# A four-layer hybrid model on one Trainium2 core: the residual stream by tokens instead of by features, and the FFN's output product by seven products of quarters

## The chip, the cores and the metric

The kernel runs on one core of one Trainium2 chip. The metric is the device time of one execution in microseconds. Before the change it was 2659.95 us, the median of three runs (2656.53 to 2660.51).

## The reference, cut to what matters

512 tokens of width 1024 go through four layers. Each layer is a mixer (RWKV-7, sliding-window attention, a gated spatial unit, gated linear attention) and an FFN, each behind an RMS norm and added to the residual stream `h`. All is float32.

```python
for i in range(DEPTH):                       # DEPTH = 4
    hn = rmsnorm(h, norm_mix[i])
    m = [rwkv7_mix, swa_sink_mix, sgu_chunk_mix, gla_mix][i](hn, ...)
    h = h + m
    h = h + swiglu(rmsnorm(h, norm_ffn[i]), ffn_w_in[i], ffn_w_out[i])
return rmsnorm(h, norm_final)

def rmsnorm(x, g):                           # over the 1024 features of a token
    return x * lax.rsqrt(jnp.mean(jnp.square(x), -1, keepdims=True) + 1e-5) * g
def swiglu(x, w_in, w_out):                  # w_in 1024 x 5632, w_out 2816 x 1024
    gate, up = jnp.split(x @ w_in, 2, axis=-1)
    return (jax.nn.silu(gate) * up) @ w_out
```

## The kernel before, in words

**Products.** A float32 product is made of three fp32r matmuls: each operand is split into a high part (a cast on ScalarE) and a low part (the rest, a subtraction on VectorE), and `mm3` multiplies high by high, high by low and low by high. Weights come by DMA into `wraw` tiles of 128 x 1024 (pool `wr`, eight buffers) and are split into `whi` and `wlo` (pools `wh` and `wl`, three buffers each).

**Residual stream.** `h` lies by features: eight tiles of 128 features x 512 tokens, two in each buffer of the pool `hp`. `out_proj` goes over the eight feature tiles: `gemm` multiplies one with the weights as the stationary operand and 512 tokens moving, `residual` adds the PSUM bank to `h[n]`, and after a stage's last product `norm_tile` prepares the next norm of that tile: a square on ScalarE, an add of it into the tile `acc` on GpSimd, and the scaled operand `h * g`, split in two. `rstd` then transposes `acc` by four blocks on PE, reduces it on VectorE, and takes the reciprocal root by three Newton steps; the factor per token is applied later, to results.

**FFN.** Its hidden width of 2816 is cut into six blocks (`WIDTHS`: four of 512, two of 384), and the blocks into three parts of two (`PARTS`). `hidden` makes gate and up of a block by `seven`: with input features and tokens halved, the four quarters of the weights (gate and up by feature half) and of the input give eight products, of which seven of sums of quarters suffice (the Strassen-Winograd scheme). The products are called m1, m2, m5, m6, m3, m7, m4 in the order made, with left operands x11, x12, s5, s6, s3, s7, x22. Sums of weight quarters are made by accumulating DMAs, issued by GpSimd: raw tile `b` takes quarters 2, 0, 3 and 1 one after another, tile `c` takes 3 and then 2. Left operands for an input are made once, by `fast_tile`, when the norm is prepared (`fast`). m1, m6, m7 and m4 accumulate in the same two PSUM banks and are read between. After each part, `out_proj` multiplies its hidden features by all eight k-tiles (six in the last part), in the plain way.

**Order.** Instructions are recorded as a program; `Program.run` puts each engine's in an order of its own by simulating the engines with a price per instruction (`price`): among ready instructions it takes the one that starts earliest, by program order within 60 ns. Up to 700 instructions ahead may be moved forward, if buffers allow. `keep_warm` fills idle PE time with products of the identity. All instructions are issued from line 233 (those fillers from line 453), so the profile's groups are told apart by tile names: `slot` are general 128 x 512 tiles (46 of them, `SLOTS`), `left` those of the FFN's results, `ps` the eight PSUM banks.

Of the kernel before, what the change touches and what calls it, by code (L numbers as in the profile page):

```python
# [17 lines left out]
P = 128  # L18
# [7 lines left out]
SLOTS = 46  # L26
# [7 lines left out]
VECS = ("norm_mix", "rw_mu", "rw_w0", "rw_a0", "rw_k_k", "rw_k_a", "rw_r_k", "norm_ffn", "norm_final", "sw_b_qkv", "sw_b_o", "sg_b_u", "sg_b_o", "gla_b_a",  # L34
# [402 lines left out]
class K:  # L437
# [3 lines left out]
    def __init__(self, prog, d, es):  # L441
# [16 lines left out]
        self.nx = []  # L458
        self.fast = False
# [13 lines left out]
    def stream(self, slots):  # L473

        self.acc = self.pool("acc", 1, side="right").tile([P, S], F32, name="acc")
        self.weight_pools(8, 3, side="right")
        self.big = self.pool("big", slots, side="right")
# [6 lines left out]
    def load_x(self, h):  # L484
        for k in range(KT):
            self.nc.sync.dma_start(h[k], self.d['x_t'][k * P:(k + 1) * P, :])

# [83 lines left out]
    def norm_tile(self, k, g):  # L571

        nc = self.nc
        last = g is self.v['norm_final']
        if k == 0:
            nc.scalar.activation(self.acc, self.h[k], AF.Square)
        else:
            sq = self.slot()
            nc.scalar.activation(sq, self.h[k], AF.Square)
            (nc.vector if last else nc.gpsimd).tensor_add(self.acc, self.acc, sq)  # L580
        if last:
            self.nx.append(self.slot())
            nc.scalar.activation(self.nx[k], self.h[k], AF.Identity, scale=g(k))
            return
        if self.fast:
            self.fast_tile(k, g)
            return
        xh, xl = self.pair()
        nc.scalar.activation(xh, self.h[k], AF.Identity, scale=g(k))
        nc.vector.scalar_tensor_tensor(xl, self.h[k], g(k), xh, op0=ALU.mult, op1=ALU.subtract)  # L590
        self.nx.append((xh, xl))

    def fast_tile(self, k, g):

        nc = self.nc
        x = self.slot()
        nc.scalar.activation(x, self.h[k], AF.Identity, scale=g(k))
        j, H = k % 4, S // 2  # L600
        a, b = slice(0, H), slice(H, S)
        if k < 4:
            if k % 2 == 0:
                self.x11 = self.pair()
            c = slice(k % 2 * H, k % 2 * H + H)
            one = tuple(t[:, c] for t in self.x11)
            self.split(x[:, a], *one)
            self.nx.append([one, x])
            return
        one, y = self.nx[j]  # L610
        two = self.pair()
        self.split(x, *two)
        f, g = self.slot(), self.slot()
        nc.vector.tensor_sub(f[:, a], x[:, b], y[:, b])
        nc.vector.scalar_tensor_tensor(f[:, b], f[:, a], -1.0, y[:, a], op0=ALU.mult, op1=ALU.subtract)
        nc.vector.tensor_sub(g[:, a], y[:, a], y[:, b])
        nc.vector.scalar_tensor_tensor(g[:, b], f[:, b], -1.0, x[:, a], op0=ALU.mult, op1=ALU.subtract)
        fs, gs = self.pair(), self.pair()
        self.split(f, *fs)
        self.split(g, *gs)  # L620
        half = lambda p, c: tuple(t[:, c] for t in p)
        self.nx[j] = dict(x11=one, x12=half(two, a), x22=half(two, b), s5=half(fs, a), s6=half(fs, b), s7=half(gs, a), s3=half(gs, b))
# [13 lines left out]
    def rstd(self, copy=True, spread=True):  # L636

        nc = self.nc
        ps = self.bank()
        for b in range(NB):  # L640
            nc.tensor.transpose(ps[:, b * P:(b + 1) * P], self.acc[:, b * P:(b + 1) * P], self.ident)
        ms = self.sm.tile([P, NB], F32, name="ms")
        nc.vector.tensor_reduce(ms, self.blocks(ps), axis=AX.X, op=ALU.add)
# [8 lines left out]
        if not copy:  # L652
            return col, ps
# [4 lines left out]
    def operand(self):  # L658
        x, self.nx = self.nx, []
        return x  # L660

    def residual(self, k, ps, bias=None):
        nc = self.nc
        if bias is None:
            nc.vector.tensor_add(self.h[k], ps, self.h[k])
        else:
            nc.vector.scalar_tensor_tensor(self.h[k], ps, bias, self.h[k], op0=ALU.add, op1=ALU.add)


    def ffn(self, i, g_next):  # L670


        nc, d = self.nc, self.d
        col, _ = self.rstd(spread=False)
        neg = self.sm.tile([P, NB], F32, name="ncol")
        nc.vector.tensor_scalar(neg, col, -1.0, None, op0=ALU.mult)
        x = self.operand()
        done = 0
        for n, part in enumerate(PARTS):
            gs = []  # L680
            for j in part:
                w = d['ffn_w_a'][i, j] if j < 4 else d['ffn_w_b'][i, j - 4]
                m = WIDTHS[j] // P
                oo = [self.pair() for _ in range(m)]
                gs += oo
                self.hidden(w, WIDTHS[j], x, col, neg, oo)
            last = n == len(PARTS) - 1
            self.out_proj(d['ffn_w_out'][i][:, :, done * P:(done + len(gs)) * P], gs, None, g_next if last else None)
            done += len(gs)

    def seven(self, w, W, x):
# [7 lines left out]
        nc = self.nc  # L699

        def load(q):
            t = []
            for u in range(2):
                raw = self.wr.tile([P, 1024], F32, name="wraw")[:, :2 * W]
                nc.sync.dma_start(raw, w[q * 2 + u])
# [3 lines left out]
        def add(a, q):  # L709
            for u in range(2):  # L710
                nc.gpsimd.dma_start(a[u], w[q * 2 + u], accum_op=ALU.add)

        def mm(key, ps, raw, first, last):
            for u in range(2):
                hi = self.wh.tile([P, 1024], F32R, name="whi")[:, :2 * W]
                lo = self.wl.tile([P, 1024], F32R, name="wlo")[:, :2 * W]
                self.split(raw[u], hi, lo)
                for b in range(2):
                    t = slice(b * P, (b + 1) * P)
                    for k in range(2):  # L720
                        xh, xl = x[u * 2 + k][key]
                        c = slice(k * W, (k + 1) * W)
                        self.mm3(ps[b], xh[:, t], xl[:, t], hi[:, c], lo[:, c], first and u + k == 0, last and u + k == 2)
# [27 lines left out]
    def hidden(self, w, W, x, col, neg, oo):  # L751
# [10 lines left out]
        def give(up, half):  # L762
# [3 lines left out]
            for j0 in range(0, W // P, 2):  # L766
# [5 lines left out]
                for j in range(n):  # L772
                    c = slice(half * 256, half * 256 + 256)
                    self.split(ps[:, j * 256:j * 256 + 256], oo[j0 + j][0][:, c], oo[j0 + j][1][:, c])
        for name, ps in self.seven(w, W, x):
# [22 lines left out]
    def out_proj(self, w, x, bias, g_next):  # L798
        for n in range(KT):
            def ev(ps):  # L800
                self.residual(n, ps, bias(n) if bias else None)
                if g_next is not None:
                    self.norm_tile(n, g_next)
            self.gemm(w[n], x, ev)
# [31 lines left out]
    def rwkv(self, g, g_next, slots):  # L836
# [24 lines left out]
        self.acc = self.slot()  # L861
# [829 lines left out]
```

## Time and profile before

| | before |
|---|---|
| median of three runs | 2659.95 us |
| profiled execution, its own time | 2662.47 us |
| its span, first to last instruction | 2660.6 us |
| instructions | 34154 |
| PE busy | 2566.0 us, 12950 products and transposes |
| VectorE, ScalarE, GpSimd busy | 1669.7, 1233.9, 434.3 us |
| granted PE clock, mean | 0.989 |
| moved by DMA | 318.47 MB, of which 92.29 MB by GpSimd's queue |

Busy times are unions of an engine's recorded durations; matmuls overlap, so the distance between starts, not the mean duration, is the price of one. In the windows, each row has the busy time of PE, PE's weight loads, VectorE, ScalarE and GpSimd with their instruction counts, then the granted clock, the DMA engines' mean share and GB/s.

### The profile page before, as it was taken

Reading aid. Unit: us, or ns where it says so; the run is one execution under the profiler, and the core shown is the slowest. Engines: PE = TensorE matmul, PEld = TensorE weight load, DVE = VectorE, ACT = ScalarE, POOL = GpSimd, SP = SyncE. Lnnn points to the kernel's source line nnn. Section 1 sums busy time; section 2 is a strip of 40 time slices with the busy share of each in tenths; the row PEclk is TensorE's granted clock in tenths of the full one; section 3 lists DMA queues with packets and bytes.
Section 4 is the critical chain, followed back from the end, with each engine's and each line's share of the span. In section 5 each row is a group of like instructions: output and inputs, shape, how many; then the busy total and the mean of one; then the engine's idle time right before and its main releaser. Section 6 shows DMA issues by size and latency. Waiting matters only on the chain. (4 is left out here: it accounts for less than half of the span.)

```text
span 2660.6 us, 34154 instructions
## 1 busy us (share of the span) xinstructions
PE 2566.0 (96%) x12950; PEld 2101.2 (79%) x12950; DVE 1669.7 (63%) x2591; ACT 1233.9 (46%) x2047; POOL 434.3 (16%) x431
## 2 busy tenths in 40 slices
PE   8999889979999999999999999999999999999998
PEld 7677677768889865788898888888888777788897
DVE  8686787576466766855556474764646645764555
ACT  4545443356354555644444232553535523553443
POOL 1022343221111233201111000110111000211010
PEclk9999999999999999999999999999999999999999
DMA  3210001168576521667674222384856221576662
GB/s 126 78 60 11 7 9 38 43 161 201 141 176 155 141 81 43 153 182 180 149 179 155 96 88 94 103 199 139 203 126 167 88 72 64 138 186 153 172 151 78
DMA packets 108580, 318.47 MB, mean 120 GB/s; under 512 B 12016, under 2 KB 19568, under 8 KB 108416
## 3 DMA queue, kind: packets, MB, share of 16 engines
q1 hardware_dynamic: 80768, 224.01, 25.5%
q0 software_dynamic: 27648, 92.29, 19.9%
q8 instruction: 101, 1.65, 0.3%
q14 instruction: 63, 0.52, 0.1%
HBM read 311.80 MB, written 2.10 MB: 118 GB/s over the span
## 5 line engine op out<-in xcount | busy, mean ns | idle before, releaser
L233 PE MATMUL ps<-whi,slot 128*128 128x512 f32 (+1 forms) x3328 | 996.9, 378 | 4.2 <-ACT left L233 3.0
L233 ACT CAST whi<-wraw 128x1024 fp32r<-128x1024 f32 (+3 forms) x566 | 558.3, 987 | 844.3 <-PE ps L233 675.3
L233 DVE TENSOR_TENSOR wlo<-wraw,whi 128x1024 fp32r<-128x1024 f32 (+2 forms) x562 | 645.6, 1149 | 409.8 <-ACT whi L233 407.0
L233 PE MATMUL ps<-slot,whi 128*128 128x512 f32 x2784 | 871.1, 392 | 1.6 <-ACT slot L233 1.6
L233 PEld LDWEIGHTS ps<-whi,slot 128*128 128x128 f32 x3328 | 617.4, 188 | 99.5 <-ACT left L233 4.8
L233 PE MATMUL ps<-wlo,slot 128*128 128x512 f32 (+1 forms) x1664 | 627.9, 377 | 4.3 <-DVE wlo L233 4.0
L233 PEld LDWEIGHTS ps<-slot,whi 128*128 128x128 f32 x2784 | 515.6, 187 | 122.6 <-issue 7.0
L233 PE MATMUL ps<-slot,wlo 128*128 128x512 f32 x1392 | 544.0, 391 | 0.0
L233 PEld LDWEIGHTS ps<-wlo,slot 128*128 128x128 f32 x1664 | 312.8, 188 | 57.7 <-DVE wlo L233 11.5
L233 PEld LDWEIGHTS ps<-slot,wlo 128*128 128x128 f32 x1392 | 259.8, 187 | 57.8 <-issue 2.5
L233 DVE TENSOR_TENSOR h<-ps,h 128x512 f32<-128x512 f32 x128 | 88.4, 691 | 283.9 <-PE ps L233 283.8
L233 POOL DMA_DIRECT2D wraw<-ffn_w_a x128 | 111.1, 868 | 655.2 <-DVE wlo L233 345.0
L233 POOL TENSOR_TENSOR acc<-acc,slot 128x512 f32<-128x512 f32 x49 | 74.2, 1514 | 654.3 <-ACT slot L233 654.2
L233 DVE TENSOR_TENSOR slot<-slot 128x512 fp32r<-128x512 f32 (+8 forms) x177 | 131.6, 754 | 23.3 <-ACT slot L233 21.2
L233 ACT COPY left<-ps 128x512 f32<-128x512 f32 (+1 forms) x196 | 108.2, 555 | 78.3 <-PE ps L233 78.2
L233 DVE TENSOR_TENSOR slot<-ps,slot 128x256 fp32r<-128x256 f32 (+3 forms) x271 | 98.3, 416 | 69.3 <-PE ps L233 41.1
L233 POOL DMA_DIRECT2D wraw<-ffn_w_b x64 | 55.2, 864 | 383.8 <-DVE wlo L233 184.7
L233 ACT CAST slot<-ps 128x256 fp32r<-128x256 f32 (+1 forms) x240 | 65.6, 365 | 46.1 <-PE ps L233 41.8
L233 DVE SCALAR_TENSOR_TENSOR left<-left,ncol 128x512 f32<-128x512 f32 (+1 forms) x96 | 65.4, 701 | 9.9 <-ACT left L233 9.9
L233 ACT CAST slot<-slot 128x512 fp32r<-128x512 f32 (+1 forms) x80 | 45.8, 576 | 48.4 <-DVE slot L233 47.6
L233 PE MATMUL ps<-slot 64*128 64x256 f32 (+4 forms) x256 | 58.3, 406 | 7.8 <-DVE slot L233 5.3
L233 DVE TENSOR_TENSOR left<-ps,left 128x512 f32<-128x512 f32 (+1 forms) x96 | 58.4, 638 | 7.9 <-PE ps L233 7.9
(257 smaller groups left out, 2359.0 us busy)
## 6 DMA issues: line engine op xcount, KB each, us to landing
wraw<-ffn_w_a SPq DMA_DIRECT2D x128, 512.0 KB, 3.5
wraw<-ffn_w_a POOLq DMA_DIRECT2D x128, 512.0 KB, 5.7
wraw<-ffn_w_out SPq DMA_DIRECT2D x64, 512.0 KB, 4.0
wraw<-ffn_w_b SPq DMA_DIRECT2D x64, 384.0 KB, 3.1
wraw<-ffn_w_b POOLq DMA_DIRECT2D x64, 384.0 KB, 6.2
wraw<-ffn_w_out SPq DMA_DIRECT2D x32, 384.0 KB, 4.7
wraw<-sg_w_v SPq DMA_DIRECT2D x16, 512.0 KB, 3.6
wraw<-sg_w_u SPq DMA_DIRECT2D x16, 512.0 KB, 3.3
```

Source lines behind the costliest of these rows:

```text
L233: op = self.add(eng.name, lambda: getattr(eng.target, what)(*map(real, args), **{k: real(a) for k, a in kw.items()}), *self.price(eng.name ...
```

## The change

`h` becomes token-major: four tiles of 128 tokens x 1024 features, loaded from `x`, and the kernel's output is token-major too. Output products of the mixers go by `gemm_tok` (tokens stationary, 512 weight columns moving, all k-tiles into four banks); the rwkv one by 256 columns and two k-tiles at a time. Biases are added as broadcast rows by GpSimd at a mixer's start. The FFN's output product goes through `seven` too, with tokens halved, the part's hidden features halved (one block each) and output features halved; its left operands are made per part from the hidden results, and each of the seven results is added to or subtracted from one quarter of `h`. Norms: `finish` takes the square sums of two token blocks and 512 features with ScalarE's accumulated output, and makes the next stage's features by PE transposes of `h` into PSUM, scaled on ScalarE. `acc`, `norm_tile` and `residual` go. `SLOTS` is 48 and the pool `left` 16.

```diff
-SLOTS = 46
+SLOTS = 48
...
+    def finish(self, half, nh):
...
+        c = slice(nh * S, nh * S + S)
+        bs = (2 * half, 2 * half + 1)
+        for b in bs:
             sq = self.slot()
+            nc.scalar.activation(sq, self.h[b][:, c], AF.Square, accum_out=self.ss[:, 2 * b + nh:2 * b + nh + 1])
+        if self.kind == 'final':
+            for b in bs:
+                nc.vector.tensor_mul(self.h[b][:, c], self.h[b][:, c], self.g[nh])
             return
+        t = slice(half * 256, half * 256 + 256)
+        for u in range(2):
+            ps = self.bank()
+            for j in range(2):
+                k = nh * 4 + u * 2 + j
+                for i, b in enumerate(bs):
+                    nc.tensor.transpose(ps[:, (j * 2 + i) * P:(j * 2 + i + 1) * P], self.h[b][:, k * P:(k + 1) * P], self.ident)
...
+                xh, xl = self.nx[k]
+                nc.scalar.activation(xh[:, t], src, AF.Identity, scale=self.g(k))
+                nc.vector.scalar_tensor_tensor(xl[:, t], src, self.g(k), xh[:, t], op0=ALU.mult, op1=ALU.subtract)
+        if self.kind == 'fast':
+            self.quarter(self.xq, self.nf, (nh, half), keep=True)
...
+    def combine(self, q, name):
...
+        x11, x12, x21, x22 = q[0, 0], q[1, 0], q[0, 1], q[1, 1]
+        if name == 's5':
+            q['s'] = [self.slot()[:, :t.shape[-1]] for t in x21]
+        for u in range(len(x11)):
+            if name == 's5':
+                nc.vector.tensor_sub(q['s'][u], x22[u], x21[u])
+            elif name == 's6':
+                nc.vector.scalar_tensor_tensor(q['s'][u], q['s'][u], -1.0, x11[u], op0=ALU.mult, op1=ALU.subtract)
+            elif name == 's3':
+                nc.vector.scalar_tensor_tensor(q['s'][u], q['s'][u], -1.0, x12[u], op0=ALU.mult, op1=ALU.subtract)
+            else:
+                nc.vector.tensor_sub(x21[u], x11[u], x21[u])
+        return x21 if name == 's7' else q['s']
...
+            w = d['ffn_o_a'][i, n] if n < 2 else d['ffn_o_b'][i]
+            self.out_fast(w, W // P, lambda key: self.left_of(gs, key), n == len(PARTS) - 1)
...
+    def out_fast(self, w, nsub, x, last):
...
+        where = {'m1': [(0, 0, 1)], 'm2': [(0, 0, 1)], 'm5': [(1, 1, -1)], 'm6': [(0, 1, -1)], 'm3': [(0, 1, -1)],
+                 'm7': [(1, 1, -1)], 'm4': [(1, 0, 1)]}
+        for name, ps in self.seven(w, S, x, nsub):
+            for half, nh, sign in where[name]:
+                for b in range(2):
+                    c = self.h[half * 2 + b][:, nh * S:(nh + 1) * S]
+                    (nc.vector.tensor_add if sign > 0 else nc.vector.tensor_sub)(c, c, ps[b])
+                if last and name in ('m2', 'm3', 'm7', 'm4'):
+                    self.finish(half, nh)
...
-                    self.split(ps[:, j * 256:j * 256 + 256], oo[j0 + j][0][:, c], oo[j0 + j][1][:, c])
...
+                t = self.slot()[:, :n * 256]
+                nc.scalar.copy(t, ps[:, :n * 256])
+                gs.setdefault((kh, half), []).append(t)
...
+    def out_proj(self, w, x, last=True):
...
+        for nh in range(2):
+            c = slice(nh * S, nh * S + S)
+
+            def ev(b, ps):
+                self.nc.vector.tensor_add(self.h[b][:, c], ps, self.h[b][:, c])
+                if last and b % 2:
+                    self.finish(b // 2, nh)
+            self.gemm_tok(w, nh * S, x, ev)
...
     def store(self):
...
+        col, _ = self.rstd(spread=False)
+        for b in range(NB):
+            for nh in range(2):
+                c = slice(nh * S, nh * S + S)
+                o = self.slot()
+                if nh:
+                    nc.scalar.activation(o, self.h[b][:, c], AF.Identity, scale=col[:, b:b + 1])
+                else:
+                    nc.vector.tensor_scalar(o, self.h[b][:, c], col[:, b:b + 1], None, op0=ALU.mult)
+                nc.sync.dma_start(self.d['out'][b * P:(b + 1) * P, c], o)
```

More of the change, by code (lines that the diff above doesn't have):

```diff
@@ new lines, in finish, with parts, quarter @@
+        if self.kind == 'fast':
+            self.quarter(self.xq, self.nf, (nh, half), keep=True)
+    LEFT = {(0, 0): 'x11', (1, 0): 'x12', (1, 1): 'x22'}
+    def parts(self, ts):
+        out = []
+        for t in ts:
+            n = t.shape[-1]
+            hi, lo = self.pair()
+            self.split(t, hi[:, :n], lo[:, :n])
+            out.append((hi[:, :n], lo[:, :n]))
+        return out
+    def quarter(self, q, out, key, keep):
+        if key in self.LEFT:
+            out[self.LEFT[key]] = self.parts(q[key])
+        if len(q) == 4 and all(len(v) == len(q[0, 0]) for v in q.values()):
+            for n in ('s5', 's6', 's7', 's3'):
+                out[n] = self.parts(self.combine(q, n))
@@ L967, in rwkv @@
                 ahead(n + 1)
-        self.h = self.eight()
-        self.load_x(self.h)
+        self.load_h()
         self.rwkv_out_proj(oo, 0, 6)
@@ L974, in rwkv @@
         self.stream(slots)
[L975 to L980 removed]
+        self.begin(g_next)
+        self.out_proj(d['rw_w_o'][6 * P:, :], oo[6:])
         ex.close()
```

281 lines of the change are left out of this document (120 added, 161 removed).

## The prediction

> **What bounds the kernel now.** I read the page first, then the windows cut at the stage boundaries, then the timeline inside one FFN, then the groups, the DMA issues and the chain of waits.
>
> ```profile
> span 2660.6 us, 34154 instructions
> ...
> PE 2566.0 (96%) x12950; PEld 2101.2 (79%) x12950; DVE 1669.7 (63%) x2591; ACT 1233.9 (46%) x2047; POOL 434.3 (16%) x431
> ```
>
> PE is busy nearly always, so a gain has to come from PE's work or from the 95 us in which it idles. The windows (columns: stretch, its length, busy time of each engine, granted clock, DMA share, GB/s) tell where those are:
>
> ```profile
> 594.00:620.00 26.00, 25.25 (x109) 20.74 (x110) 16.34 (x21) 16.01 (x23) 4.29 (x5) 0.93 0.88 199
> 620.00:880.00 260.00, 260.00 (x1247) 223.00 (x1246) 149.81 (x196) 120.44 (x175) 33.51 (x41) 1.00 0.69 164
> 880.00:910.00 30.00, 29.68 (x146) 25.36 (x145) 21.17 (x30) 15.88 (x28) 3.92 (x3) 1.00 0.54 173
> 910.00:1075.00 165.00, 155.06 (x721) 107.63 (x720) 114.45 (x214) 90.97 (x248) 57.56 (x49) 1.00 0.23 71
> 1075.00:1140.00 65.00, 63.12 (x287) 51.70 (x286) 52.26 (x78) 41.58 (x60) 14.56 (x14) 1.00 0.71 173
> ...
> 1700.00:1765.00 65.00, 63.29 (x288) 52.05 (x287) 51.18 (x77) 42.22 (x59) 15.12 (x14) 1.00 0.68 166
> ...
> 2280.00:2340.00 60.00, 57.86 (x260) 47.17 (x259) 47.17 (x71) 36.98 (x52) 13.08 (x13) 1.00 0.67 156
> ```
>
> The body of an FFN (620 to 880) has PE busy for 260.00 of 260 us while VectorE stands at 58%, ScalarE at 46% and DMA at 0.69. The passage from an FFN into a mixer (880 to 910) loses 0.3 us. The passage from a mixer into an FFN (the four windows around 600, 1100, 1730, 2310) loses 0.75, 1.88, 1.71 and 2.14 us, 6.5 together: there the square sums in acc end late. So an FFN is bound by the number of PE instructions, and the price of one is its distance from the next:
>
> ```profile
> 779.31 1.23 DVE L233 TENSOR_TENSOR wlo<-wraw,whi 128x1024 fp32r<-128x1024 f32 x1 [0.20 <-ACT whi L233]
> ...
> 780.46 1.05 ACT L233 CAST whi<-wraw 128x1024 fp32r<-128x1024 f32 x1 [1.18 <-PE ps L233]
> ...
> 784.71 0.69 PEld L233 LDWEIGHTS ps<-ident,left 128*128 128x128 f32 x6 [0.17 <-DVE left L233]
> 784.82 0.82 PE L233 MATMUL ps<-ident,left 128*128 128x128 f32 x6
> ...
> 787.30 0.62 PE L233 MATMUL ps<-slot,whi 128*128 128x512 f32 x2
> ...
> 787.75 0.39 PE L233 MATMUL ps<-slot,wlo 128*128 128x512 f32 x1
> ...
> 787.98 0.62 PE L233 MATMUL ps<-slot,whi 128*128 128x512 f32 x2
> ```
>
> Three 512-column products lie between 787.30 and 787.98: 0.227 us each. Six transposes' weight loads take 0.69 us: 0.115 each, or 0.11 from start to start when the last one's own length (140 ns, group row below) is taken off and the rest divided by five.
>
> **The change, PE first.** (a) An FFN's output product took 22 k-tiles x 8 output tiles x 3 = 528 products of 512 columns. By quarters it is 7 x 2 token blocks x (4+4+3) k-tiles x 3 = 462. Four FFNs: 264 fewer x 0.227 = -59.9 us, all of it on PE's path, since nothing else ends last there. (b) Features now come by transposes: 32 at each of the seven norms that feed a stage, 224 x 0.11 = +24.6. (c) Four transposes of acc at each of eight norms and four that spread the final column go: 36 x 0.11 = -4.0. Net -39.3 us. The mixers' output products keep their count (192 for 8 k-tiles either way). The rwkv one becomes 288 products of 256 columns for 144 of 512. A product of 256 columns is not in the trace; half of 0.227 is 0.113 and a weight load can follow the last after 0.11, so I take 0, with 144 x 0.11 = 16 us as the far end should weight loads hold it up.
>
> **What the other engines get.** The groups (busy, mean ns of one, idle before and its releaser):
>
> ```profile
> L233 DVE TENSOR_TENSOR slot<-slot 128x512 fp32r<-128x512 f32 (+8 forms) x177 | 131.6, 754 | 23.3 <-ACT slot L233 21.2
> L233 DVE TENSOR_TENSOR slot<-ps,slot 128x256 fp32r<-128x256 f32 (+3 forms) x271 | 98.3, 416 | 69.3 <-PE ps L233 41.1 <-ACT slot L233 28.0
> L233 DVE TENSOR_TENSOR h<-ps,h 128x512 f32<-128x512 f32 x128 | 88.4, 691 | 283.9 <-PE ps L233 283.8
> L233 POOL TENSOR_TENSOR acc<-acc,slot 128x512 f32<-128x512 f32 x49 | 74.2, 1514 | 654.3 <-ACT slot L233 654.2
> L233 ACT CAST slot<-ps 128x256 fp32r<-128x256 f32 (+1 forms) x240 | 65.6, 365 | 46.1 <-PE ps L233 41.8 <-DVE slot L233 4.1
> L233 PEld LDWEIGHTS ps<-ident,left 128*128 128x128 f32 x352 | 43.2, 140 | 11.1 <-DVE left L233 3.0
> L233 ACT ACTIVATE slot<-h 128x512 f32<-128x512 f32 x57 | 35.9, 630 | 19.4 <-DVE h L233 16.8 <-DMA h<-x_t 1.5
> ```
>
> VectorE's recorded durations overlap, as its own timeline shows:
>
> ```profile
> 878.63 0.95 DVE L233 TENSOR_TENSOR wlo<-wraw,whi 128x768 fp32r<-128x768 f32 x1
> 879.49 0.55 DVE L233 TENSOR_TENSOR left<-ps,left 128x384 f32<-128x384 f32 x1
> 879.96 1.14 DVE L233 SCALAR_TENSOR_TENSOR left<-left,ncol 128x384 f32<-128x384 f32 x2
> ...
> 883.92 1.08 DVE L233 TENSOR_TENSOR slot<-ps,slot 128x256 fp32r<-128x256 f32 x3
> 884.92 1.01 DVE L233 TENSOR_TENSOR left<-left 128x384 f32<-128x384 f32 x2
> ...
> 893.97 0.69 DVE L233 TENSOR_TENSOR h<-ps,h 128x512 f32<-128x512 f32 x1 [1.52 <-PE ps L233]
> 894.61 0.96 DVE L233 TENSOR_TENSOR wlo<-wraw,whi 128x768 fp32r<-128x768 f32 x1
> ```
>
> From start to start: 768 columns 0.86, 384 columns 0.47, 256 columns out of PSUM 0.33, the residual add 0.64. The first two give 0.08 us and 1.02 ns a column, so 0.60 for 512 and 1.12 for 1024 (estimates). One full output product (K = 1024) then gives VectorE 14 weight splits (8 before) x 1.12 = 15.7, 14 operand splits x 0.60 = 8.4, 8 sums of quarters x 0.62 = 5.0 and 14 residual adds x 0.64 = 9.0: 38.1 us beside 168 x 0.227 = 38.1 us of PE. That is level, but x11's and x12's splits (2.4) and three weight tiles (3.4, wh and wl hold three) can be made during the hidden product before it, and the residual adds of m3 and m4 (2.6) run behind it: about 30 of 38. A hidden product has 15.7 of splits and about 7 of sums for as much PE time, so over a part VectorE stands near 70%. The last part (K = 768) has 7 x 1.72 + 7 x 0.93 + 4 x 0.95 + 9.0 = 31.4 us, plus 12 of 16 feature subtractions x 0.33 = 4.0, less 6.1 ahead or behind: 29.3, beside 126 x 0.227 + 24 x 0.11 = 31.2 us of PE. Counted by recorded durations (1.23 a weight split, 0.69 the others, 0.416 out of PSUM) and with nothing ahead, it is 42.1 against 38.1 and 40.2 against 31.2: 8 x 4 + 4 x 9 = 68 us late. The near end is 0, as in the window from 620 to 880. I take +8 us (0.5 at each of eight full parts, 1 at each of four last ones), close to the near end since the work ahead and behind is there in the code; 0 to 68 is kept for the range. ScalarE takes casts and squares, and stays below VectorE. GpSimd loses acc's adds (49 x 1.5 = 74 us), and gets 96 more accumulating issues and 16 bias adds; it has 84% free, and only the issues queued behind one another matter (a rival). SP's queue gets six broadcast rows (biases, final gain) ahead of a stage's weights; the raw pool of eight tiles has those weights loaded by then, so I count nothing.
>
> **The passages.** FFN into mixer: the mixer's first product needs feature tile 0 of all tokens, which m4, the last of the seven, completes. After m4 stand the residual add 0.69, four transposes 0.44, two scaled copies 0.73, a subtraction 0.42 and four hand-overs. Hand-overs are about 0.15 each by the end's chain (below: acc ends at 2646.60, ms begins at 2647.34, with 0.44 of transposes between). That is 2.9 us, and the mixer's products are queued on PE behind those transposes, where today seven of eight feature tiles are done before the last: 3 x 3 = +9 us (0 if the row-sum or mask work fills it, 15 at twice the hand-overs). Mixer into FFN: x11 is ready half an output product early and m1, m2 (10.9 us) cover the 10 us of VectorE work ahead of s5; the 6.5 us lost there today can go, the sums for s6, s7 and s3 can cost as much: 0 (-6.5 to +10).
>
> **The end.**
>
> ```profile
> 2606.39 38.09 PE ps L233 x174
> 2644.51 0.70 DVE h L233
> 2645.90 0.70 DVE acc L233
> 2647.34 0.70 DVE ms L233
> 2651.01 0.70 DVE slot L233
> 2653.64 1.79 DVE slot L233 x3
> ```
>
> From 2644.51 to 2660.6 are 16.1 us. Now: add 0.70, square 0.63, column work at most 3.0 (2648.04 to 2651.01, which still holds the spread that goes), eight tiles on two engines 4 x 0.7 = 2.8, and the 5.2 us from the last tile to the end: 12.3 and a hand-over. -3.5.
>
> **Sum**: -39.3 + 8 + 9 + 0 - 3.5 = -25.8 us. The profiled execution took 2662.47 us (span 2660.6), which gives 2636.7; it lay 2.5 above the median of 2659.95, so 2634 is forecast for the median.
>
> **Two rules of the Trainium skill.** The rows above give a transpose 0.11 us in a burst. The Trainium skill (TensorE: Matmul & The Clock Gate, Part 4: PE-mode transpose) gives about 275 ns for one in a kernel; by that the sum would be 2671. What hangs on it is a rival below. The window from 910 to 1075 has PE idle for 9.9 us in pieces at a clock of 1.00. The same page (the table under "Why this matters for your kernels") warns of idle gaps over about 3 us, after which the clock halves; by it the three passages would each lose some 2 us more, an estimate, and the sum would be 2640.
>
> **Rivals.**
>
> *VectorE becomes the bound of the output product.* For: 38.1 beside 38.1 us, and operand splits, sums and residual adds stand in one queue, so a late add holds m4, which writes the same bank. Against: the start-to-start prices and the work ahead. Price up to 68 instead of 8: 2694. From 2.8 us at each of the twelve (34 / 12) the change is slower.
>
> *Accumulating loads come late.*
>
> ```profile
> q1 hardware_dynamic: 80768, 224.01, 25.5%
> q0 software_dynamic: 27648, 92.29, 19.9%
> ...
> wraw<-ffn_w_a POOLq DMA_DIRECT2D x128, 512.0 KB, 5.7
> wraw<-ffn_w_out SPq DMA_DIRECT2D x64, 512.0 KB, 4.0
> ```
>
> Between s5 and s6, and between s3 and s7, the next quarter is added into the same raw tile after its split: landing 5.7, cast 1.05, subtraction 1.23 make 8.0 us beside a product of 24 x 0.227 = 5.4. Today plain output products stand between such chains; after, all products have them. A packet's time is 3.03 us per MB plain and 5.74 accumulating (shares x 2660.6 / MB), so the 11.5 MB that each FFN adds are 66 us in about 340, and 0.69 becomes 0.9. If no split runs ahead: 2.5 x 2 x 12 = 60 us, 2694. It turns the sign from 1.1 us at each place. Against: the hidden products have the same chain one behind another, with PE at 260.00 of 260.
>
> *Transposes cost their recorded time*, 0.27 us, for want of a burst (eight at a time, each group behind an add): 224 x 0.16 = +36, 2670.
>
> *All is covered*: stalls, passages and the 6.5 us vanish: -39.3 - 6.5 - 3.5, about 2611.
>
> That fewer products would run than said is not open: the counts are in the code.
>
> **Chances.** Forecast (2620 to 2648) 0.47; all covered 0.09; VectorE 0.22, spread over 2645 to 2694 (0.06 faster, 0.08 same, 0.08 slower); late loads 0.14 (0.02 same, 0.12 slower); transposes 0.05 and something unseen 0.03, both slower. Faster by over 0.2% (5.3 us, about what a measurement of this kernel can tell) 0.62, within 0.10, slower 0.28. The range 2608 to 2678 leaves out the far halves of the two slow rivals.
>
> **What would show it.** PE instructions near 13,020 (264 products fewer, 188 transposes more, 144 short products more); PE busy 260 of 260 in an FFN's body if no rival holds; VectorE below 0.9 there; DMA share about 0.9; gaps near 3 us ahead of each mixer; an end of 12 to 13 us. I am wrong if PE idles inside the output products behind `wlo` (VectorE) or `wraw` (loads), or if transposes stand 0.2 us apart.

## The result: 1.6% slower, and the profile after

The changed kernel takes 2699.34 us, the median of four runs (2694.56 to 2706.73), against 2658.24 for the kernel before (2656.21 to 2660.51; one run more than the three ahead of the change): a ratio of 1.0157, 95% interval 1.0129 to 1.0185. It is slower, and above the predicted range. The profiled execution took 2696.06 us.

From the page of the kernel after: span, engines, clock and DMA in 40 slices, queues, and the group of fillers, products of the identity that the order puts where its own simulation sees PE idle:

```profile
span 2694.4 us, 35601 instructions
...
PE 2577.9 (96%) x13324; PEld 2118.2 (79%) x13324; DVE 1825.4 (68%) x2804; ACT 1380.2 (51%) x2304; POOL 465.8 (17%) x492
...
PEclk9999999999999999999999999999999999999999
DMA  3210001268888532588896222388888221398885
...
q0 software_dynamic: 41472, 138.43, 28.8%
q1 hardware_dynamic: 85504, 225.59, 24.6%
...
L453 PE MATMUL ps<-ident 128*128 128x128 f32 x670 | 103.5, 295 | 1.7 <-POOL ident L233 1.4
```

The same group on the page of the kernel before:

```profile
L453 PE MATMUL ps<-ident 128*128 128x128 f32 x364 | 59.6, 306 | 1.5 <-POOL ident L233 1.4
```

PE's count is the 13,018 that follows from the prediction's counts and 306 fillers more (12950 - 264 + 188 + 144 + 306 = 13324). PE's 96% is therefore misleading: at about 0.112 us from start to start the new fillers alone are 34 us of PE doing nothing useful. The DMA slices of an FFN go from mostly 5 to 7 tenths to mostly 8; in the body (620 to 880) the share is 0.84, where about 0.9 was forecast. The windows of the kernel after, cut as those of before (PE, weight loads, VectorE, ScalarE, GpSimd, clock, DMA share, GB/s):

```profile
620.00:880.00 260.00, 254.13 (x1239) 218.51 (x1238) 184.61 (x233) 143.67 (x199) 47.19 (x56) 0.99 0.84 196
880.00:910.00 30.00, 27.73 (x132) 23.16 (x131) 28.34 (x45) 19.25 (x39) 9.08 (x10) 0.94 0.77 177
1100.00:1110.00 10.00, 7.13 (x44) 6.10 (x43) 9.93 (x17) 8.35 (x13) 0.00 (x0) 1.00 0.00 0
...
1330.00:1350.00 20.00, 17.32 (x78) 13.72 (x78) 13.60 (x18) 6.35 (x7) 3.43 (x4) 1.00 0.95 204
2335.00:2350.00 15.00, 12.42 (x71) 10.67 (x70) 14.73 (x28) 11.15 (x22) 0.00 (x0) 1.00 0.16 57
...
2640.00:2681.00 41.00, 36.05 (x172) 29.41 (x171) 34.28 (x55) 21.25 (x41) 5.17 (x7) 1.00 0.48 84
```

The FFN's body is no longer full (254.13 of 260, fillers counted as busy). Two kinds of places stand out: the mixer-to-FFN passages (1100 and 2335) and the FFN's last parts (880, 2640), where VectorE is busy for 84 to 99% of the time, and the end of a part inside an FFN (1330), where it stands at 68%. What PE's weight loads waited for says who was late (waits, kernel after: us in total, times, longest):

```profile
PEld ps L233 <- DVE wlo L233: 30.8, 45, 2.8
PEld ps L233 <- ACT whi L233: 30.7, 36, 2.5
...
PEld ps L233 <- ACT left L233: 8.7, 7, 2.3
```

Before, the first two were 15.2 and 9.4:

```profile
PEld ps L233 <- DVE wlo L233: 15.2, 27, 2.4
...
PEld ps L233 <- ACT whi L233: 9.4, 6, 4.7
```

So PE waits for split weights. The timeline of the kernel after, between two results of an output product, shows how a split comes late:

```profile
1330.40 0.86 POOL L233 DMA_DIRECT2D wraw<-ffn_o_a  x1 [1.49 <-DVE wlo L233]
...
1331.08 1.05 ACT L233 CAST whi<-wraw 128x1024 fp32r<-128x1024 f32 x1 [2.04 <-DMA wraw<-ffn_o_a]
...
1333.56 1.29 DVE L233 TENSOR_TENSOR slot<-slot 128x512 fp32r<-128x512 f32 x2
...
1334.76 0.68 DVE L233 TENSOR_TENSOR h<-h,ps 128x512 f32<-128x512 f32 x1
...
1335.36 0.69 DVE L233 TENSOR_TENSOR slot<-slot 128x512 fp32r<-128x512 f32 x1
...
1335.72 0.38 PE L453 MATMUL ps<-ident 128*128 128x128 f32 x2
1335.96 0.68 DVE L233 TENSOR_TENSOR h<-h,ps 128x512 f32<-128x512 f32 x1
1336.17 1.04 ACT L233 CAST whi<-wraw 128x1024 fp32r<-128x1024 f32 x1 [1.43 <-PE ps L453]
1336.56 3.49 DVE L233 TENSOR_TENSOR wlo<-wraw,whi 128x1024 fp32r<-128x1024 f32 x3
1337.27 0.73 PE L233 MATMUL ps<-whi,slot 128*128 128x512 f32 x2 [1.16 <-ACT whi L233]
...
1337.83 0.83 PE L453 MATMUL ps<-ident 128*128 128x128 f32 x6
...
1338.96 0.50 PE L233 MATMUL ps<-wlo,slot 128*128 128x512 f32 x1 [0.30 <-DVE wlo L233]
...
1341.56 1.04 ACT L233 CAST whi<-wraw 128x1024 fp32r<-128x1024 f32 x1 [4.35 <-PE ps L233]
```

Three things meet here. The first is a load: the accumulating load issued at 1330.40, which had itself waited for the split of the quarter before it, landed by the trace's record at 1336.07, and the cast at 1336.17 began 0.10 us behind it, as the one at 1331.08 did behind the load before (landed 1330.98). The second is the buffer. By the times and the program, the cast at 1331.08 and the one after it are for m4, the product behind the next, and hold two of the three buffers; the third came free when PE ended its last product on the tile before (1335.50 and 0.39), 0.2 us ahead of the landing. The view puts the cast's wait of 1.43 us down to a filler that ended at about that time. At the next cast the buffer alone was missing: its load had landed at 1338.72, and it began at 1341.56, with PE named. The third is VectorE's queue. From 1333.56 to 1336.6 it makes operand splits and residual adds; the weight splits queue behind and then come three in a row. PE starts on the cast's result as soon as it ends (1337.21), and waits again for the subtraction, by the times the second of the three.

The same can be asked of each of the 81 waits of PE's weight loads for `whi` and `wlo` (61.5 us in the kernel after), if each is paired with the cast and the subtraction that ended last before it. In 37 of them, 30.9 us, the cast had begun within 0.25 us behind the landing of a load issued by GpSimd (such casts stand mostly 0.1 us behind it). In 20, 18.0 us, the subtraction began over 0.3 us after that cast had ended, so it stood in VectorE's queue. In the kernel before the two are 9.8 and 6.4 us.

A count from start to start over the whole trace gives the size. What exceeds 0.2275 us for a product of 512 columns, 0.1735 for 384, 0.109 for a transpose and 0.112 for a filler is a gap (2% allowed); a filler counts 0.112 besides, and gaps behind the mixers' smaller products are left out. All mixers and FFNs are in it, so only differences between rows tell something, and each row is one execution:

| kernel (experiments below) | fillers | their time | gaps | sum, us |
|---|---|---|---|---|
| before | 364 | 40.8 | 128.8 | 169.5 |
| after | 670 | 75.0 | 163.3 | 238.3 |
| output product plain | 416 | 46.6 | 128.0 | 174.6 |
| no accumulating loads | 492 | 55.1 | 144.4 | 199.5 |
| plain instead of accumulating | 670 | 75.0 | 159.5 | 234.6 |
| dearer price | 620 | 69.4 | 144.1 | 213.6 |
| four buffers alone | 462 | 51.7 | 191.4 | 243.1 |
| price, later sums, four buffers | 454 | 50.8 | 118.9 | 169.7 |
| price, later sums, five buffers | 414 | 46.4 | 107.8 | 154.2 |
| five buffers, last part plain | 312 | 34.9 | 88.6 | 123.6 |
| before, price and five buffers | 342 | 38.3 | 112.7 | 151.0 |

From before to after 69 us were lost, half of them in fillers. That is more than the 60 that the missing products save, and with the transposes' 20.5 and 2.5 for the shorter rwkv products the sum is 32 us; the spans differ by 33.8.

### The profile page after: what moved, and what is told of

Read it like the earlier page. It is cut to its first block, busy times and chain, and to the rows that moved or that the text cites. A ratio compares the mean times of both kernels' runs of the same rounds, so it can differ in the third digit from the quotient of the medians.

```text
span 2694.4 us, 35601 instructions
## 1 busy us (share of the span) xinstructions
PE 2577.9 (96%) x13324; PEld 2118.2 (79%) x13324; DVE 1825.4 (68%) x2804; ACT 1380.2 (51%) x2304; POOL 465.8 (17%) x492
## 3 DMA queue, kind: packets, MB, share of 16 engines
q0 software_dynamic: 41472, 138.43, 28.8%
## 5 line engine op out<-in xcount | busy, mean ns | idle before, releaser
L233 PE MATMUL ps<-whi,slot 128*128 128x512 f32 (+1 forms) x5072 | 1556.2, 384 | 28.7 <-ACT whi L233 20.5
L233 PEld LDWEIGHTS ps<-whi,slot 128*128 128x128 f32 x5072 | 944.7, 189 | 196.1 <-ACT whi L233 28.4
L233 ACT CAST whi<-wraw 128x1024 fp32r<-128x1024 f32 (+2 forms) x632 | 626.9, 993 | 741.6 <-PE ps L233 543.3
L233 PE MATMUL ps<-wlo,slot 128*128 128x512 f32 (+1 forms) x2536 | 975.9, 385 | 17.0 <-DVE wlo L233 16.5
L233 PEld LDWEIGHTS ps<-wlo,slot 128*128 128x128 f32 x2536 | 478.6, 189 | 108.6 <-DVE wlo L233 30.2
L233 PE MATMUL ps<-slot,whi 128*128 128x512 f32 (+2 forms) x864 | 274.6, 396 | 2.0 <-ACT slot L233 1.9
L233 DVE TENSOR_TENSOR slot<-slot 128x512 fp32r<-128x512 f32 (+5 forms) x369 | 234.4, 662 | 26.8 <-ACT slot L233 24.8
L233 PEld LDWEIGHTS ps<-slot,whi 128*128 128x128 f32 (+2 forms) x864 | 157.0, 185 | 47.6 <-issue 6.2
L233 PE MATMUL ps<-slot,wlo 128*128 128x512 f32 (+2 forms) x432 | 169.7, 393 | 0.0
L233 DVE TENSOR_TENSOR h<-h,ps 128x512 f32<-128x512 f32 x168 | 112.5, 683 | 21.2 <-PE ps L233 20.3
```

Source lines behind the costliest of these rows:

```text
L233: op = self.add(eng.name, lambda: getattr(eng.target, what)(*map(real, args), **{k: real(a) for k, a in kw.items()}), *self.price(eng.name ...
```

## The experiments

Each ratio is to the kernel before, run on the same chip, with its 95% interval; before took 2667 to 2670 us there, so ratios are compared and not times. A difference of two ratios, given in us, is uncertain by some 7 to 14 us.

**Which half costs: the output product plain, the stream token-major.** `PLAIN = (0, 1, 2)` names the parts whose output product goes through `out_proj`, as the mixers' do.

```diff
+            if n in PLAIN:
+                r0 = sum(WIDTHS[:part[0]])
+                self.out_proj(d['ffn_w_out'][i][r0:r0 + len(flat) * P, :], flat, n == len(PARTS) - 1)
+                continue
```

> The FFN's output product is plain again in all parts (three matmuls per k-tile, no quarters, no accumulating loads for it); the token-major residual, the transposes and ScalarE's square sums stay. This splits the loss between the two halves of the change. It has 264 products more than the changed kernel (+60 us of PE). If the loss lies inside the output products (late loads or VectorE; some 15 us of idle PE and fillers per FFN, 60 in all), it takes about 2699 + 60 - 60 = 2699 or less. If the loss lies in the token-major residual and the passages between stages, the time rises to 2740 or more. From the kernel before, the token-major part alone should cost 20 us of transposes: 2680 if nothing else is wrong with it.

1.0082 (1.0057 to 1.0108): 22 us, beside 188 transposes x 0.109 = 20.5. The token-major stream costs its transposes and hardly more. Gaps and fillers are those of the kernel before but for 5 us. The output product by quarters, which should have given 60 us back, made it slower still: it adds 64 us of them (174.6 to 238.3).

**Only the last part plain**, `PLAIN = (2,)`:

> As the changed kernel, but the last part's output product (K = 768) is plain, with the next norm's features made behind it as in a mixer; parts one and two stay by quarters. 72 products more (+16 us of PE). If most of the loss is at the end of an FFN, where norm work and the accumulating loads of six k-tiles come together, it falls to 2670 to 2685. If the loss is spread evenly over the output products, a third of it goes and the time stays at 2690 to 2700.

1.0094 (1.0064 to 1.0124), against 1.0157 (1.0129 to 1.0185): some 17 us faster (6 to 28) although it runs 72 products more (four FFNs x 18, 16 us). So the seven products of the last parts lost more than the 16 us that they save.

**Who is late: the accumulating loads of the output product left out** (s5, s6 and x22 then meet the same quarter, and so do s3 and s7):

```diff
         def add(a, q):
+            if not sums:
+                return
```

> As the changed kernel, but the accumulating loads of the output product are left out: its raw tiles are split again without the added quarter (so the quarter sums of the output weights are missing). Nothing else changes. Late loads: the 46 MB less on the DMA engines and the shorter chain between s5 and s6, s3 and s7 give back most of the loss inside the output products, 40 to 60 us: 2640 to 2660. VectorE bound: within 10 us of the changed kernel, 2690 to 2700.

0.9951 (0.9933 to 0.997), some 55 us faster than the kernel after, with an order of its own. The loads then became plain ones. Every engine's sequence of instructions is that of the kernel after, fillers included, so that only the loads' length changes; the sums are left out by this too:

```diff
-                nc.gpsimd.dma_start(t, w[q][:, k * W:(k + n) * W], accum_op=ALU.add)
+                nc.gpsimd.dma_start(t, w[q][:, k * W:(k + n) * W])
```

> As the changed kernel, but each accumulating load of the output product becomes a plain load of the same bytes from the same queue into the same tile (so the quarter sums of the output weights are missing, as in e2_no_sums). The chain split, load, split stays; only the price of the load falls (shares of the 16 DMA engines: about 3.0 us per MB plain, 5.6 accumulating). If the DMA engines' time for accumulating is what makes the loads late, it keeps more than half of what e2_no_sums gained: ratio to the kernel before 0.995 to 1.005. If it is the length of the chain itself (split, issue, landing, split), it stays near the changed kernel: 1.010 to 1.016.

1.0134 (1.0093 to 1.0176): 6 us better, within the uncertainty. The page of this kernel shows that they did land sooner (KB each, us to landing), 4.2 for 5.6:

```profile
wraw<-ffn_o_a POOLq DMA_DIRECT2D x64, 512.0 KB, 4.2
```

PE's waits behind a landing fall from 30.9 to 10.6 us, but all its waits for split weights only from 61.5 to 51.4, since those in VectorE's queue rise (18.0 to 22.5), and the 670 fillers stand in the order whether a load is late or not. So shorter transfers alone do not help; what the order lays around a tile that is loaded again after its split counts for more.

**VectorE: the left operands' low part left out** (the high part stands in, and half the slots are used):

```diff
-        return self.parts(q[at[key]] if key in at else self.combine(q, key))
+        out = []
+        for t in q[at[key]] if key in at else self.combine(q, key):
+            hi = self.slot(F32R)[:, :t.shape[-1]]
+            self.nc.scalar.copy(hi, t)
+            out.append((hi, hi))
+        return out
```

> As the changed kernel, but the left operands of the output product get no low part: 154 subtractions of up to 512 columns per FFN less on VectorE (some 8 us per full output product), the high part stands in for it, with as many matmuls. VectorE bound: the loss inside the output products goes, 40 to 60 us: 2640 to 2660. Late loads: within 10 us of the changed kernel, 2690 to 2700.

1.0014 (0.9995 to 1.0033), between the two expectations. (It leaves out 42 subtractions per FFN, not 154: VectorE's count falls by 168.) Was it VectorE's time or the slots? In the next kernel the slots are taken as in the kernel after, and GpSimd sets the low part to zero:

```diff
+            hi, lo = [v[:, :t.shape[-1]] for v in self.pair()]
+            self.nc.scalar.copy(hi, t)
+            self.nc.gpsimd.memset(lo.bitcast(F32), 0.0)
```

> As the changed kernel, but the low part of each left operand of the output product is set to zero by GpSimd instead of being made by VectorE (that part of the product is missing). Against e3_no_low, which also needed half the operand slots, this takes only VectorE's time away. If VectorE's time was the cause of e3_no_low's gain (38 us), it gains as much: ratio 0.998 to 1.005. If the slots were, it stays near the changed kernel: 1.010 to 1.018.

1.0016 (0.9995 to 1.0037): VectorE's time, with the order that is laid anew around it (498 fillers for 670). In the first of these kernels it falls by 91.5 us (1825.4 to 1733.9), and the kernel by some 38.

**Sums on GpSimd in place of loads.** Two of the four sums of quarters add two raw tiles on GpSimd, first in the output products, then in the hidden products too:

```diff
+        def sum2(a, b, q):
+            if not (out):
+                return add(a, q)
+            for t, o in zip(a, b):
+                nc.gpsimd.tensor_add(t, t, o)
```

> As the changed kernel, but in the output product two of the four sums of weight quarters are made by GpSimd in SBUF (quarter 2 + quarter 0 from the tile of m1, and + quarter 3 from the tile that is loaded for m3) instead of by accumulating loads: 23 MB less accumulated, same result. Late loads: half of what e2_no_sums gained, 25 us: ratio 1.004 to 1.009. VectorE bound: GpSimd's adds slow VectorE's subtractions beside them, no gain or worse: 1.014 to 1.025.

> As e7_pool_out, but in the hidden products too: 69 MB less accumulated in all, 24 x 4 more adds on GpSimd of about 2.4 us. Late loads: more than e7_pool_out's gain, ratio 0.995 to 1.006. VectorE bound: worse than e7_pool_out, 1.02 or more.

1.046 (1.0413 to 1.0508) and 1.0872 (1.0819 to 1.0925): far slower than either branch expected. Groups of the first (busy, mean ns), and two weight splits in its timeline:

```profile
L233 DVE TENSOR_TENSOR wlo<-wraw,whi 128x1024 fp32r<-128x1024 f32 (+2 forms) x628 | 768.1, 1228 | 530.8 <-ACT whi L233 528.6
...
L233 POOL TENSOR_TENSOR wraw<-wraw 128x1024 f32<-128x1024 f32 (+1 forms) x48 | 122.9, 2569 | 278.2 <-DVE wlo L233 196.0
```

```profile
639.12 6.73 DVE L233 TENSOR_TENSOR wlo<-wraw,whi 128x1024 fp32r<-128x1024 f32 x2
```

A sum takes 2.57 us and stands between two splits like the load. The weight splits on VectorE take 1.228 us on average for 1.161, and this is the work of a few: the 15 of 1024 columns that overlap a sum take 3.40 us each, the other 470 take 1.24 as before. PE's waits for `wlo` grow from 30.8 to 64.6 us. The raw tiles that are added are held longer too, and what that costs was not separated.

**The order: what it believes of an accumulating load.** The price in the simulated order is doubled; nothing is left out. By the code, 512 KB on an idle queue then land after 5.51 us of simulated time instead of 4.06; the record has 5.6:

```diff
-            op.columns = 4.0 * math.prod(views[0].shape)
+            op.columns = (8.0 if 'accum_op' in kw else 4.0) * math.prod(views[0].shape)
```

> As the changed kernel, but the program that sets the instruction order prices an accumulating load at twice a plain one on the DMA engines (it priced both alike). Only the order changes. If the loss comes from an order made for loads that land sooner than they do, the waits on late weight tiles become fewer: 10 to 30 us less, ratio 1.004 to 1.012. If the engines are short of time or the chain too long whatever the order, within 8 us: 1.013 to 1.018.

1.0021 (1.0001 to 1.0041), some 36 us faster by the order alone, more than expected. Casts that begin within 0.25 us behind a landing fall from 108 to 43, and PE's waits behind one from 30.9 to 6.5 us. The same line in the kernel before:

> The kernel before, with accumulating loads priced at twice a plain one when the order is made, as in e6_price. If the old price hurts only where all FFN products are made of quarters, nothing moves: 0.998 to 1.002. If it hurts wherever there are accumulating loads, this gains 0.5% or more, and e6_price's gain says nothing of the change.

0.9944 (0.9924 to 0.9964). So 15 of the 36 us are to be had in any case, and about 21 are peculiar to the change. That the truer price is what helps is not shown: with plain loads the output product's transfers landed about when the old price said, and little came back. An order with more slack before each reload would explain both. On top of the dearer price, the FFN's operands s5, s6, s3 and s7 are recorded where first used:

```diff
-            for n in ('s5', 's6', 's7', 's3'):
-                out[n] = self.parts(self.combine(q, n))
+            out['later'] = q
```

> As e6_price, and in addition the FFN's own sums of quarters (s5, s6, s3, s7) are recorded where the first hidden product uses them, in that order, instead of all at once when the last features are finished, so that VectorE's splits of the first weights stand ahead of them. Same result. If VectorE's queue at the passage from mixer to FFN is what idles PE there (2.6 us of waiting and some 3 us of fillers at each of four), it is 12 to 24 us faster than e6_price: ratio 0.993 to 0.998. If PE waits there for something else, it stays at 1.000 to 1.004.

0.9985 (0.9968 to 1.0002): 10 us more (3 to 17), a little under what was expected. The edit bears on the mixer-to-FFN passage, where the chain of waits of the kernel after had VectorE's sums and splits ahead of the first weight split (start, us, what):

```profile
2336.68 3.11 DVE slot L233 x5
2339.82 1.31 DVE slot L233 x2
2341.15 2.57 DVE slot L233 x5
2344.16 1.89 DVE slot L233 x3
2346.12 0.65 DVE wlo L233
```

**Room to run ahead.** Four buffers for `whi` and `wlo`, paid with three slots and two tiles of `left`, on top of price and later sums:

```diff
-SLOTS = 48
+SLOTS = 45
-        self.weight_pools(8, 3, side="right")
+        self.weight_pools(8, 4, side="right")
-            k.left = k.pool("left", 16)
+            k.left = k.pool("left", 14)
```

> As e10_price_lazy, with four buffers instead of three for the high and low weight parts, so that splits can run one more tile (12 products, 2.7 us) ahead of PE; paid for with three slots and two buffers of the pool left. If the wait chain load, split, load, split is short of room to run ahead, 10 to 20 us faster than e10_price_lazy: 0.988 to 0.994. If slots are what is short, slower than it.

0.9847 (0.9821 to 0.9872). The same lines without price and later sums:

> The changed kernel with four buffers instead of three for the high and low weight parts, old prices, old place of the sums; three slots and two left buffers fewer. If the run-ahead of the splits is the cause of the loss, most of the 41 us come back: ratio 0.995 to 1.003. If e11's gain came from the three edits together, it stays above 1.008.

1.0098 (1.0063 to 1.0134), only some 16 us. The waits of this kernel show what held it:

```profile
PEld ps L233 <- DVE left L233: 21.6, 27, 5.0
PEld ps L233 <- ACT left L233: 21.3, 6, 6.3
...
PEld ps L233 <- DVE wlo L233: 15.8, 16, 2.8
PEld ps L233 <- ACT whi L233: 13.0, 15, 2.7
```

The waits for split weights fall from 61.5 to 28.8 us, as the fourth buffer should make them, but those for `left` rise from 11.8 to 42.9. In the kernel with price and later sums the latter are 5.6 (3.2 and 2.4). Room and order give more together than apart, and no run has the fourth buffer with 16 `left` tiles.

Would the kernel before profit as much? It gets price and four buffers (44 slots), then five (and six raw tiles):

> The kernel before with four buffers for the weight parts (44 slots instead of 46) and the new price of accumulating loads. If three buffers are short only for an output product by quarters, it stays where e9_before_price was, 0.992 to 0.997, and e11 (0.985) beats it by some 20 us: the change pays once it has the room. If it falls to 0.985 or below, the room helps any order and the change itself brings nothing.

> The kernel before with five buffers for the weight parts, six raw tiles (what space allows), 44 slots and the new price. Its plain output products have less to split, so the room should bring little beyond e13: 0.988 to 0.994, and the change is worth about 1% (e14 against it). If it falls to 0.982 or below, the change is worth nothing even with room.

0.9918 (0.9889 to 0.9946) and 0.9916 (0.9895 to 0.9938): no more than some 7 us beyond the price alone, and nothing from the fifth. Next, five buffers in the changed kernel (43 slots, seven raw tiles), and the last part plain with four and with five:

> As e11_four_parts with five buffers for the weight parts, seven raw tiles instead of eight and 43 slots. If run-ahead is still short: 5 to 15 us faster than e11, 0.979 to 0.983. If four are enough, or a raw tile less holds the loads back: 0.985 to 0.995.

> As e11_four_parts, with the last part's output product plain (16 us of PE more, as in e4_last_plain). If the last part is still held up by VectorE and the loads with norm work beside them, it is level with e11 or faster: 0.980 to 0.985. If four buffers cured that too, it is some 10 us slower: 0.987 to 0.991.

> As e14_five, with the last part's output product plain as in e15. If the last part's loss comes from something else than missing room, the gains of e14 and e15 over e11 (0.4 and 0.3%) add up: ratio 0.975 to 0.979. If both cure the same loss, it is no faster than e14: 0.980 to 0.985.

0.9805 (0.9776 to 0.9833), 0.9815 (0.9787 to 0.9844), and 0.9738 (0.9717 to 0.976), a median of 2596.35 us. The last beats both kernels: price, later sums, five buffers, and seven products in all but an FFN's last part. Across the second FFN, windows of the kernel after, of the one with five buffers and all parts by quarters, and of the last, whose largest wait for split weights follows:

```profile
1200.00:1350.00 150.00, 146.10 (x665) 119.07 (x665) 104.22 (x122) 77.44 (x98) 25.56 (x30) 1.00 0.85 196
...
1200.00:1350.00 150.00, 150.00 (x736) 130.34 (x735) 105.29 (x128) 88.60 (x123) 30.04 (x36) 1.00 0.91 215
...
1200.00:1350.00 150.00, 150.00 (x753) 132.26 (x752) 106.79 (x134) 87.42 (x125) 29.05 (x35) 1.00 0.91 218
```

```profile
PEld ps L234 <- ACT whi L234: 3.8, 15, 0.9
```

PE is full again, with VectorE at 70.2 and 71.2% (69.5% in the kernel after) and DMA at 0.91 (0.85). The change as such, against the kernel before with the same price and five buffers, is worth about 1.1% (0.9805 to 0.9916), and 1.8% with the last part plain; the later sums, which the kernel before did not get, are within that.

## Why the prediction was wrong, point by point

**The step that failed** is the term "I take +8 us (0.5 at each of eight full parts, 1 at each of four last ones)", and its reason, "the work ahead and behind is there in the code". Between the kernel with the plain output product and the kernel after, which differ in the output product alone, gaps and fillers grew by 64 us. Some 9 of them were forecast for the passages into the mixers (below), so the term is nearer 55 than 8. The prediction kept 68 as its far end, on recorded durations with nothing ahead; that end was near in size, but not for its reason, since VectorE was never too slow as a whole. That VectorE's and PE's sums of work are equal (38.1 and 38.1 us) was read as level, with 30 us left after what can be made ahead. What counts at each product is whether the next weight tile is split when PE reaches it, and of PE's waits for split weights half stood behind a landing and three tenths behind VectorE's queue. "wh and wl hold three" is the place: a weight tile serves 168 / 14 = 12 products, 2.7 us, and with one in use at most two stand ready, 5.4 us; at 1336 both were held for a later product. One reload of a raw tile (8.0 us by the prediction's own sum), or VectorE's queue of the moment (3 us at 1333.56, and three splits behind it), uses that up.

**The reference case was misread.** The window 620 to 880 of before had PE at 260.00, and the prediction took it as showing that hidden products can stand one behind another. They could, with plain output products between them: with these back, gaps and fillers return to within 5 us of before. That the order catches up in the plain products is my reading. The prediction wrote this down in the rival on loads, and then set it aside.

**The rivals.** *VectorE becomes the bound* (0.22) and *accumulating loads come late* (0.14) were priced at 2694 each, and the profiled run took 2696. They are not two cases. Taking VectorE's work away gave 38 us, the loads 55, the order's price 36: each relieves the same path (reload, cast, subtraction, product), and the gains overlap. The load rival named the right place, where 30.9 of 61.5 us of waits lie, but its price "landing 5.7" alone is not the cause, since landing at 4.2 in the same order gave almost nothing. Nor is VectorE full: 71% in the body (184.61 of 260), below the 0.9 that was to mark it.

**Mixer-to-FFN passages**, 0 in the sum with +10 as the far end: PE busy is down 2.87 us of 10 at 1100 and 2.58 of 15 at 2335, fillers counted as busy, and later sums gave 10 us over four, so the far end was nearer than 0. **FFN into mixer**, 2.9 us each, was right at the first passage, shown here in the timeline of the kernel after; the other two were not timed:

```profile
918.80 0.39 PE L233 MATMUL ps<-whi,slot 128*128 128x512 f32 x1
919.02 0.38 PE L453 MATMUL ps<-ident 128*128 128x128 f32 x2
...
921.92 0.49 PE L233 MATMUL ps<-slot,whi 128*128 128x512 f32 x1 [0.19 <-ACT slot L233]
```

From the end of the FFN's last product (918.80 and 0.227) to the mixer's first are 2.9 us, with eight transposes and twelve fillers in it.

**Right.** Transposes cost their burst price (timeline of the kernel after):

```profile
545.00 1.94 PE L233 MATMUL ps<-ident,h 128*128 128x128 f32 x16
```

Less the last one's 0.276 us, 1.66 us for fifteen is 0.111 each. The 275 ns that the Trainium skill (TensorE: Matmul & The Clock Gate, Part 4: PE-mode transpose) gives is, here, the length of one (276 ns) and not its distance from the next, so that rival's 36 us did not come. (Net of the 36 transposes that go, it should have been some 30.) The mean clock did not fall either (0.990 for 0.989), though between 880 and 910 it was 0.94 for 1.00 before. The rwkv product of 256 columns costs (3.11 - 0.29) / 23 = 0.122 us, +2.5 us for 288 where 0 was taken:

```profile
526.42 3.11 PE L233 MATMUL ps<-et,rk 128*128 128x256 f32 x24
```

The count of products was right, and so were the net cost of the token-major stream (20.5 us; 22 measured) and the end (last addition at 2680.91 to 2694.4, 13.5 us, against 12.3 and a hand-over).

**What stays open.** Why leaving the loads out gives 55 us and making them plain some 6 is not separated further: without them both the order and the wait behind the split go at once. Plain loads were not run with an order laid anew for them. The shares of price, room and VectorE cannot be added up: they come to more than the 69 us lost.

## What to carry to other kernels

When a change takes work from a full engine and gives some to engines that are half idle, ask at each step whether the next operand is ready, not whether the sums of work fit: with VectorE at 71% in an FFN's body the kernel lost 69 us behind three buffers, and PE was full again at 70% behind five with a better order. A tile that is loaded, split and loaded again is a chain; give it room, and a price in the planner that fits the recorded landing, before judging the algorithm. When a view puts a wait down to an engine, look at what landed just before it ended. Count fillers as idle time, and take as a reference a stretch that already has the new sequence, not one with easier work between.

## What the runs showed of the hardware

- An accumulating load of 512 KB lands 5.6 us after its issue and the same load without accumulation, in the same order and queue, 4.2 us.
- GpSimd's addition of two 128x1024 float32 tiles takes 2.57 us, twice VectorE's subtraction of that size (1.23 us), and the 15 weight splits on VectorE that overlap one take 3.40 us each.
- A product of 256 columns comes every 0.122 us, a little over half of the 0.227 of one with 512.
